# Batched matmul on one core: loads and stores moved from SyncE's DMA queue to GpSimd's, one packet per DMA engine

## The chip, the core and the metric

The kernel runs on one core of one Trainium2 chip. The metric is the device time of one execution in microseconds (us); the median of several runs is given. A profile of one execution comes with it.

## What is computed

For each of 32 batches the result is the matrix product of a 256 x 512 matrix and a 512 x 384 matrix, all in float32:

```python
batch, dim_i, dim_j, dim_k = 32, 256, 512, 384
x: (batch, dim_i, dim_j) float32
y: (batch, dim_j, dim_k) float32
return np.einsum('bij,bjk->bik', x, y).astype(np.float32)
```

In and out together, 54.5 MB pass between the chip's main memory (HBM) and the on-chip buffer (SBUF): 512 KB of x, 768 KB of y and 384 KB of results per batch.

## The kernel before

One batch is one step of the loop. `load(b)` brings x[b] and y[b] into SBUF with two DMAs: each of the 128 partitions gets two rows of x (4 KB, contiguous in HBM) and four rows of y (6 KB). `compute(b)` then does the following. ScalarE (ACT) and VectorE (DVE) cast the four row groups of y to float16, two each (`y_r`, L61 and L63). TensorE (PE) transposes x in eight 128 x 128 blocks by a multiplication with an identity matrix (L69), and DVE and ACT copy these from PSUM to SBUF as float16 (`xt_sb`, L71 and L73). Eight matmuls of 128 x 128 by 128 x 384 follow (L82), which add up four steps of j for each half of the rows, and ACT and DVE copy the two halves to `o_sb` (L91, L93). `store(b, o_sb)` writes 3 KB per partition back with one DMA (L97).

Loads run six batches ahead of the compute (`AHEAD`); x and y have nine buffers each, `o_sb` has eight. Before the loop the kernel issues the loads of batches 0 to 5; GpSimd (POOL) builds the identity matrix meanwhile. In the loop the load of batch b+6 is issued first, then the store of batch b. All 96 DMAs are issued by SyncE (SP), whose queue works in order: x(0), y(0), ..., x(6), y(6), store(0), x(7), y(7), store(1) and so on, with the stores of batches 25 to 31 at the end. A DMA is spread over the 16 DMA engines, eight partitions to each. The framework gives the DMAs eight completion semaphores in turn, so that from the ninth on each issue waits until the DMA eight places earlier has landed; a store waits for its `o_sb` as well, and a load for its buffer.

POOL does nothing after the identity matrix is built.

Of the kernel before, what the change touches and what calls it, by code (L numbers as in the profile page):

```python
# [1 line left out]

# [5 lines left out]


MM_DT = mybir.dt.float16  # L10
F32 = mybir.dt.float32
P = 128
AHEAD = 6


@with_exitstack
def kernel(
    ctx: ExitStack,
    tc: tile.TileContext,
    x: bass.AP,  # L20
    y: bass.AP,
    out: bass.AP,
):
    nc = tc.nc

    B, I, J = x.shape
    _, _, K = y.shape

    NI = I // P
    NJ = J // P  # L30

    const_pool = ctx.enter_context(tc.tile_pool(name="const", bufs=1))
    x_pool = ctx.enter_context(tc.tile_pool(name="x_pool", bufs=AHEAD + 3))
    y_pool = ctx.enter_context(tc.tile_pool(name="y_pool", bufs=AHEAD + 3))
    yr_pool = ctx.enter_context(tc.tile_pool(name="yr_pool", bufs=4))
    xt_pool = ctx.enter_context(tc.tile_pool(name="xt_pool", bufs=4))
    o_pool = ctx.enter_context(tc.tile_pool(name="o_pool", bufs=8))
    tpsum_pool = ctx.enter_context(tc.tile_pool(name="tpsum", bufs=4, space=bass.MemoryType.PSUM))
    opsum_pool = ctx.enter_context(tc.tile_pool(name="opsum", bufs=4, space=bass.MemoryType.PSUM))

    identity = const_pool.tile([P, P], F32)

    loaded = {}

    def load(b):


        x_sb = x_pool.tile([P, NI, J], F32, name="x_sb")
        y_sb = y_pool.tile([P, NJ, K], F32, name="y_sb")
        x_src = x[b].rearrange("(p r) j -> p r j", p=P)  # L50
        y_src = y[b].rearrange("(q t) k -> q t k", q=P)
        nc.sync.dma_start(out=x_sb, in_=x_src)  # L52
        nc.sync.dma_start(out=y_sb, in_=y_src)  # L53
        loaded[b] = x_sb, y_sb

    def compute(b):
        x_sb, y_sb = loaded.pop(b)
        y_r = yr_pool.tile([P, NJ, K], MM_DT, name="y_r")
        for t in range(NJ):
            if t % 2 == 0:  # L60
                nc.scalar.copy(y_r[:, t], y_sb[:, t])  # L61
            else:
                nc.vector.tensor_copy(y_r[:, t], y_sb[:, t])  # L63

        xt_sb = xt_pool.tile([P, NJ, NI, P], MM_DT, name="xt_sb")
        for t in range(NJ):
            t_ps = tpsum_pool.tile([P, NI, P], F32, name="t_ps")
            for r in range(NI):
                nc.tensor.transpose(t_ps[:, r], x_sb[:, r, t::NJ], identity)  # L69
            if t % 2 == 0:  # L70
                nc.vector.tensor_copy(xt_sb[:, t], t_ps)  # L71
            else:
                nc.scalar.copy(xt_sb[:, t], t_ps)  # L73

        o_sb = o_pool.tile([P, NI, K], F32, name="o_sb")
        o_ps = [
            opsum_pool.tile([P, K], F32, name=f"o_ps_{r}", tag="o_ps")
            for r in range(NI)
        ]
        for t in range(NJ):  # L80
            for r in range(NI):
                nc.tensor.matmul(  # L82
                    o_ps[r],
                    xt_sb[:, t, r],
                    y_r[:, t],
                    start=(t == 0),
                    stop=(t == NJ - 1),
                )
        for r in range(NI):
            if r % 2 == 0:  # L90
                nc.scalar.copy(o_sb[:, r, :], o_ps[r])  # L91
            else:
                nc.vector.tensor_copy(o_sb[:, r, :], o_ps[r])  # L93
        return o_sb

    def store(b, o_sb):
        nc.sync.dma_start(  # L97
            out=out[b].rearrange("(p r) k -> p r k", p=P), in_=o_sb
        )

    HEAD = 2
    load(0)
    load(1)
    make_identity(nc, identity)
    for b in range(HEAD, AHEAD):
        load(b)
    for b in range(B):
        if b + AHEAD < B:
            load(b + AHEAD)
        store(b, compute(b))  # L110


# [1 line left out]
_INS = ['x', 'y']  # L114
_OUTS = [((32, 256, 384), 'float32')]


# [23 lines left out]
```

## Time and profile before

| | |
|---|---|
| three runs | 137.07, 137.32, 137.32 us (median 137.32) |
| the profiled execution | 137.07 us, of which the span of the trace is 135.3 us |
| granted TensorE clock, mean | 0.992 of full speed |
| busy: PE, DVE, ACT, POOL | 85.9, 63.3, 68.9, 0.7 us |
| DMA | 54.64 MB, mean 404 GB/s over the span |
| from issue to landing, median | x 10.2 us, y 11.2 us, store 10.9 us |
| one issue on SP's queue | 0.33 us in the steady part, 0.38 to 0.46 at the start |

The profile is one execution's record. Busy time is the time in which an engine worked; an engine that isn't the bottleneck may idle for free. The slices divide the span into 40 equal parts, and the DMA row gives the busy share of the 16 DMA engines in tenths. The chain goes back from the last instruction to what released each step. Matmuls are pipelined and the ends of their records are modelled.

### The profile page before, as it was taken

Reading aid. Unit: us, or ns where it says so; the run is one execution under the profiler, and the core shown is the slowest. Engines: PE = TensorE matmul, PEld = TensorE weight load, DVE = VectorE, ACT = ScalarE, POOL = GpSimd, SP = SyncE. Lnnn points to the kernel's source line nnn. Section 1 sums busy time; section 2 is a strip of 40 time slices with the busy share of each in tenths; the row PEclk is TensorE's granted clock in tenths of the full one; section 3 lists DMA queues with packets and bytes.
Section 4 is the critical chain, followed back from the end, with each engine's and each line's share of the span. In section 5 each row is a group of like instructions: output and inputs, shape, how many; then the busy total and the mean of one; then the engine's idle time right before and its main releaser. Section 6 shows DMA issues by size and latency. Waiting matters only on the chain.

```text
span 135.3 us, 1733 instructions
## 1 busy us (share of the span) xinstructions
PE 85.9 (63%) x512; PEld 59.4 (44%) x512; DVE 63.3 (47%) x160; ACT 68.9 (51%) x161; POOL 0.7 (1%) x6
## 2 busy tenths in 40 slices
PE   0599777777745676565676565677565677565640
PEld 0457455555424454344454344454344454344420
DVE  0237555554436544446544456544446544446520
ACT  3246666664446454646454646454546444546520
POOL 2000000000000000000000000000000000000000
PEclk9999999999999999999999999999999999999996
DMA  4999999999999999999999999999999999999993
GB/s 166 408 420 418 417 415 397 410 412 421 410 423 414 416 420 421 421 427 413 419 420 419 419 420 422 424 416 419 420 419 423 414 417 419 422 421 416 413 392 149
DMA packets 13833, 54.64 MB, mean 404 GB/s; under 512 B 1536, under 2 KB 1536, under 8 KB 13824
## 3 DMA queue, kind: packets, MB, share of 16 engines
q1 hardware_dynamic: 13824, 54.53, 98.8%
q8 instruction: 4, 0.07, 0.2%
q14 instruction: 5, 0.04, 0.1%
HBM read 41.94 MB, written 12.58 MB: 403 GB/s over the span
## 4 chain that ended last, share of the span: by engine, by line
DMA 73%; PE 12%; DVE 5%; ACT 4%; SPq 2%; issue 1%; ACTq 0%
DMA y_sb<-in_y_dram 40%; DMA out_dram<-o_sb 33%; PE o_ps L82 10%; DVE xt_sb L71 3%; ACT y_r L61 3%; DVE y_r L63 2%; PE t_ps L69 1%; ACT o_sb L91 1%; SPq L52 1%; DVE o_sb L93 1%; SPq L53 1%; ACT xt_sb L73 0%; ACTq L61 0%
## 5 line engine op out<-in xcount | busy, mean ns | idle before, releaser
L82 PE MATMUL o_ps<-y_r,xt_sb 128*128 128x384 f16 x256 | 48.2, 331 | 35.2 <-ACT y_r L61 30.6
L82 PEld LDWEIGHTS <-xt_sb 128*128 128x128 f16 x256 | 25.0, 98 | 51.9 <-issue 35.7
L69 PE MATMUL t_ps<-identity,x_sb 128*128 128x128 f32 x256 | 39.2, 297 | 8.9 <-DMA x_sb<-in_x_dram 8.8
L69 PEld LDWEIGHTS t_ps<-identity,x_sb 128*128 128x128 f32 x256 | 34.7, 210 | 18.3 <-PE o_ps L82 13.4
L93 DVE COPY o_sb<-o_ps 128x384 f32<-128x384 f32 x32 | 17.8, 558 | 42.7 <-PE o_ps L82 42.7
L61 ACT CAST y_r<-y_sb 128x384 f16<-128x384 f32 x64 | 29.7, 510 | 13.3 <-DMA y_sb<-in_y_dram 13.3
L73 ACT CAST xt_sb<-t_ps 128x256 f16<-128x256 f32 x64 | 23.6, 373 | 18.5 <-PE t_ps L69 16.4
L91 ACT COPY o_sb<-o_ps 128x384 f32<-128x384 f32 x32 | 15.3, 479 | 29.0 <-PE o_ps L82 29.0
L63 DVE CAST y_r<-y_sb 128x384 f16<-128x384 f32 x64 | 20.1, 356 | 20.0 <-DMA y_sb<-in_y_dram 20.0
L71 DVE CAST xt_sb<-t_ps 128x256 f16<-128x256 f32 x64 | 26.6, 423 | 4.6 <-PE t_ps L69 4.1
L61 ACT ACT_TABLE_LOAD x1 | 1.3, 1283 | 0.7 <-PEq L125 0.7
masks.py:199 POOL TENSOR_SCALAR_AFFINE_SELECT identity<-identity 128x128 f32<-128x128 f32 x1 | 0.3, 294 | 0.1
masks.py:197 POOL MEMSET identity<- 128x128 f32 x1 | 0.2, 205 | 0.3 <-POOLq L125 0.3
L125 POOL MEMSET const-bfloat16-1.0<- 128x1 bf16 x1 | 0.1, 102 | 0.0
L125 POOL MEMSET const-uint8-127<- 128x1 uint8 x1 | 0.1, 102 | 0.0
L125 POOL MEMSET const-float32-0.0<- 128x1 f32 x1 | 0.1, 99 | 0.2 <-issue 0.2
L125 POOL MEMSET const-float32-1.0<- 128x1 f32 x1 | 0.1, 99 | 0.0
## 6 DMA issues: line engine op xcount, KB each, us to landing
y_sb<-in_y_dram SPq DMA_DIRECT2D x32, 768.0 KB, 11.2
x_sb<-in_x_dram SPq DMA_DIRECT2D x32, 512.0 KB, 10.2
out_dram<-o_sb SPq DMA_DIRECT2D x32, 384.0 KB, 10.9
```

The costliest lines, as they stand in the source:

```text
L52: nc.sync.dma_start(out=x_sb, in_=x_src)
L53: nc.sync.dma_start(out=y_sb, in_=y_src)
L61: nc.scalar.copy(y_r[:, t], y_sb[:, t])
L63: nc.vector.tensor_copy(y_r[:, t], y_sb[:, t])
L69: nc.tensor.transpose(t_ps[:, r], x_sb[:, r, t::NJ], identity)
L71: nc.vector.tensor_copy(xt_sb[:, t], t_ps)
L73: nc.scalar.copy(xt_sb[:, t], t_ps)
L82: nc.tensor.matmul(o_ps[r], xt_sb[:, t, r], y_r[:, t], start=(t == 0), stop=(t == NJ - 1),)
L91: nc.scalar.copy(o_sb[:, r, :], o_ps[r])
L93: nc.vector.tensor_copy(o_sb[:, r, :], o_ps[r])
L125: nc = _bacc.Bacc("TRN2", target_bir_lowering=False, num_devices=1)
```

## The change

The loads of batches 0 and 1 stay on SP's queue. All later loads and all stores are issued by POOL, in the same order as before, and with `single_packet=True`: the pieces that a DMA gives to one DMA engine (eight, one per partition) form one packet. The bytes, the tiles, the buffers and the compute stay as they were. The semaphores come in two groups now: SP's four DMAs use the first four of one group, and POOL's 92 DMAs go round eight of their own, so that POOL's first eight (loads 2 to 5) wait for no earlier DMA. POOL's issues stand behind the building of the identity matrix. The lines after the edit move by four: the casts are L65 and L67, the store L101.

```diff
-        nc.sync.dma_start(out=x_sb, in_=x_src)
-        nc.sync.dma_start(out=y_sb, in_=y_src)
+        if b < HEAD:
+            nc.sync.dma_start(out=x_sb, in_=x_src)
+            nc.sync.dma_start(out=y_sb, in_=y_src)
+        else:
+            nc.gpsimd.dma_start(out=x_sb, in_=x_src, single_packet=True)
+            nc.gpsimd.dma_start(out=y_sb, in_=y_src, single_packet=True)
         loaded[b] = x_sb, y_sb
...
     def store(b, o_sb):
-        nc.sync.dma_start(
-            out=out[b].rearrange("(p r) k -> p r k", p=P), in_=o_sb
+        nc.gpsimd.dma_start(
+            out=out[b].rearrange("(p r) k -> p r k", p=P), in_=o_sb, single_packet=True
         )
 
     HEAD = 2
```

## The prediction

> **What bounds the kernel now.** I read the page first (slices, queues, chain), then the DMA queue's issues in order of time, then short windows at both ends. The page says that the DMA engines are the bound:
>
> ```profile
> DMA  4999999999999999999999999999999999999993
> GB/s 166 408 420 418 417 415 397 410 412 421 410 423 414 416 420 421 421 427 413 419 420 419 419 420 422 424 416 419 420 419 423 414 417 419 422 421 416 413 392 149
> DMA packets 13833, 54.64 MB, mean 404 GB/s; under 512 B 1536, under 2 KB 1536, under 8 KB 13824
> ...
> q1 hardware_dynamic: 13824, 54.53, 98.8%
> ...
> DMA 73%; PE 12%; DVE 5%; ACT 4%; SPq 2%; issue 1%; ACTq 0%
> ```
>
> The engines are full in every slice but the first and the last, at about 419 GB/s, and 98.8% of their time is one queue. Of its 13,824 packets 1,536 are tiny (16 engines x 96 DMAs: the completions); the other 12,288 are one per partition and DMA. So each engine handles 24 data packets a batch (8 of 4 KB for x, 8 of 6 KB for y, 8 of 3 KB for a store) and 3 completions.
>
> The issue order, in the queue of SyncE (start, length, line):
>
> ```profile
> 95.57 0.33 SPq L52 DMA_DIRECT2D x_sb<-in_x_dram  x1
> 96.48 0.33 SPq L53 DMA_DIRECT2D y_sb<-in_y_dram  x1
> 97.75 0.34 SPq L97 DMA_DIRECT2D out_dram<-o_sb  x1
> 99.60 0.33 SPq L52 DMA_DIRECT2D x_sb<-in_x_dram  x1
> ```
>
> One batch takes 99.60 - 95.57 = 4.03 us, 4.05 over longer stretches (83.40 to 99.60 is four batches), with only 1.0 us of issuing. An issue waits for the DMA eight earlier, since there are eight completion semaphores. So seven DMAs are always queued behind the one that lands, some 7 x 1.35 = 9.5 us of work. Compute isn't the bound: when PE, DVE and ACT still lag (17.1 to 30 us of the chain) they do a batch in 3.28 us. A store is late only by order: that of batch 24 is issued at 114.02, while batch 31's results are ready at 130.67, so batch 24's, seven periods earlier, at about 102.3.
>
> Both ends (columns: window, its length, busy us of PE, PEld, DVE, ACT, POOL; then clock, DMA share, GB/s):
>
> ```profile
> 2.00:3.00 1.00, 0.00 (x0) 0.00 (x0) 0.00 (x0) 0.02 (x1) 0.00 (x0) 1.00 0.80 307
> 3.00:4.00 1.00, 0.00 (x0) 0.00 (x0) 0.00 (x0) 0.00 (x0) 0.00 (x0) 1.00 1.08 428
> ...
> 131.00:132.00 1.00, 0.00 (x0) 0.00 (x0) 0.00 (x0) 0.00 (x0) 0.00 (x0) 1.00 0.86 341
> 132.00:133.00 1.00, 0.00 (x0) 0.00 (x0) 0.00 (x0) 0.00 (x0) 0.00 (x0) 1.00 0.78 310
> 133.00:134.00 1.00, 0.00 (x0) 0.00 (x0) 0.00 (x0) 0.00 (x0) 0.00 (x0) 0.61 0.37 147
> ```
>
> The engines are full from about 2.5 us and run out one by one after 131. The sum below is against the profiled execution's own 137.07 us: span 135.30 and 1.77 around it. The three runs' median is 137.32.
>
> **Part 1, the packets.** 92 DMAs (30 x, 30 y, 32 stores, about 31 batches' worth) go from one packet per partition to one per engine, eight pieces in it. Bytes and their order stay. What a packet costs beside its bytes can be read from the trace's packet records: 3, 4 and 6 KB take 121, 159 and 234 ns. The line through them is 37.7 ns per KB; 8 ns don't scale. At that slope a batch's 104 KB per engine cost 3.92 us, and a batch takes 4.05, so 0.13 us is outside the bytes (27 packets at 5 ns, neighbours overlapping a little). If this goes with packets, 21 of 27 go, or 24 if a completion rides in its packet: 0.10 or 0.12 us a batch, over 31 batches 3.2 or 3.7 us. If it goes with the pieces, not the packets, 0. The fastest of the 40 slices (427 against 419) would make 2.4 us. A loss isn't excluded, since no row shows what POOL's queue costs the engines; I allow 1 us. I take -3.2, since the constant in the records is the nearest row.
>
> The Trainium skill ("DMA: Bandwidth & Descriptors", "Why small descriptors are slow (HBM only)") puts a fixed cost of about 3 cycles on each packet and says that joining them pays only at 256 B or below. With its 850 MHz that would be an estimate of 24 x 3.5 ns x 31 = 2.6 us; its second sentence speaks against the change, but at a queue this full even 2% shows.
>
> **Part 2, issuing from GpSimd.** 92 issues leave SP (0.33 us each) for POOL, otherwise empty after 1.30 us (0.7 us busy in all). The trace has no DMA issued by POOL. Below: SP's 0.33. Above: POOL's smallest instruction is 0.10 us, and one such step per DMA engine gives 1.6 us. I take 1.0, the middle. Three a batch are 3.0 us of 4.05. Each issue again waits for the DMA eight earlier; behind it stand the next loads and stores. The cover is the seven queued DMAs, 9.5 us against 1 us more of issue: cost nothing. It ceases at 1.35 us an issue, a third of a batch's 4.05, where the engines run dry (rival B).
>
> DVE's two y_r casts a batch (356 ns each) may meet these issues; neither 0.7 us more on POOL (3.7 of 4.05) nor a cast late by 1 us is on the path while compute has 0.77 us a batch to spare.
>
> The Trainium skill ("SBUF — State Buffer", "Who interferes with whom") says that a DVE copy or cast in a two-port mode locks GpSimd out, so descriptors wait. The 128x384 cast at 356 ns is shorter than the 128x256 one from PSUM at 423, which fits a faster mode; by the page part of these 0.7 us would be added to POOL's 3.0, still under 4.05.
>
> **Part 3, the start.** Loads 0 and 1 stay on SP; SP then has nothing to wait for. Loads 2 to 5 are eight DMAs free of waits on POOL, and x and y of load 6 follow as x(2), y(2) land. Then POOL stands at the store of batch 0, and loads 7 onward stand behind it. Now two queues feed the same engines at once, which this trace never shows. Before, x(0) landed at 4.16 and y(0) at 5.98. First bytes of POOL's x(2): 1.30 + 1.0 + 0.9 (SP's own lag, 0.74 to about 1.6) = 3.2 us.
>
> Bound one: the queues share bytes evenly. y(0) lands near 8.5, batch 0's store can issue near 13, and the 9.2 MB of loads 0 to 6 keep the engines busy to 1.8 + 9.2/0.418 = 23.8. Cost 0. Bound two: they alternate packet by packet, when each 6 KB packet of y(0) waits for a whole POOL packet of 32 or 48 KB (1.2 or 1.8 us). Eight of these and its own time are some 14 us; with one packet for the rest of x(0) and 1 us to land, y(0) is there near 20. Batch 0 took 10.66 - 5.98 = 4.7 us from there to its o_sb, so its store issues near 24.6 and moves 1.9 us later, near 26.5, while the engines ran dry at 23.8: cost 2.7 us, once, because compute at 3.28 us then gains on DMA at 3.95. I take the middle, +1.3, since no row decides it.
>
> The Trainium skill ("DMA: Bandwidth & Descriptors", "Queues, rings and completion order") has the second: engines go round their queues by whole packets. By it the sum below would be 1.4 us higher.
>
> **Part 4, the end.** The last store can issue only after batch 31's o_sb (130.67 now), and it landed 3.7 us later, behind stores 25 to 30. With POOL's longer issue 0 to 0.7 us shows; I take +0.3.
>
> **The sum.** 137.07 - 3.2 + 0 + 1.3 + 0.3 = 135.5 us, 1.1% less. Own range of this case: 133.4 (3.7 off, nothing given back) to 136.8 (3.2 off, 2.7 and 0.3 back: 136.9).
>
> **Rivals.**
> A, slower by little: the constant belongs to the pieces, not the packets, and the two queues at the start alternate. For it: the number of pieces per engine stays eight. Against: the constant is the same 8 ns for all three sizes, as a boundary would be. 137.07 + 2.7 + 0.3 = 140.1 with the whole start cost, 137.6 with a fifth of it at the start and no packet gain; 1 us more if the queue itself costs. Chance 0.23.
> B, slower by much: POOL becomes the bound. Place: the in-order queue of POOL from the first wait on. Price: 31 batches x 3 x (issue - 1.35). At 1.45 us 9.3 us more (146.4); at 1.6 it would be 23 us (160). It decides from 1.35. Against: the estimate of 1.0 and 25% room. Chance 0.15.
> C, no change that can be told: packet gain (2.4 by the slices, 3.2 by the records) and whole start cost (2.7) cancel, 136.8 to 137.3. Chance 0.09.
> D, the flag does nothing on these sizes, and POOL's queue delivers as SP's did: 137.1 to 137.5. Chance 0.03, mostly in "slower".
>
> **How the numbers follow.** The forecast has 0.50, with 133.4 to 136.8 as its own range. 0.2% (0.27 us) is about what a measurement of this kernel can tell from no change. Faster: 0.50, and 0.02 from C's edge: 0.52. Same: 0.08. Slower: A, B, the rest: 0.40. For 8 in 10 the range runs from 133.2 to 142.0: it takes in the forecast, A, C, D and B's beginning (1.40 us an issue), and leaves out the rest of B and a gain over 3.7.
>
> **What would show it.** In the profile after: data packets of the software queue at 3 per engine and batch, middle slices near 429 GB/s (1.704 MB in 3.95 us) if part 1 holds, 419 if not. POOL issues at 0.7 to 1.3 us with gaps between; solid POOL issues and DMA slices below 9 mean B. In the start, y(0) landing near 8.5 or near 20, and whether a DMA slice about 24 us has a hole. Wrong from the ground up would be middle slices under 415 with POOL idle: then the engines themselves go slower on this queue.

## The result and the profile after

The changed kernel took 141.86 us (median of four runs) against 137.22 us before on the same chip: a ratio of 1.036, with an interval of 1.029 to 1.043. It is slower by 4.6 us; the forecast was 135.5. The profiled execution took 141.8 us, of which the span is 140.0, so 1.8 us lie around the span, as before. All of the difference is inside the span.

First the page of the changed kernel, the same parts as were shown of before: slices, packets, queues, and the chain that ended last.

```profile
DMA  4999999999999999999999999999999999999800
GB/s 160 407 421 422 418 414 393 425 417 418 405 421 419 426 422 424 412 422 420 421 426 425 420 425 418 422 421 415 426 425 414 421 422 421 421 423 419 328 28 0
DMA packets 11785, 54.64 MB, mean 390 GB/s; under 512 B 1536, under 2 KB 1536, under 8 KB 11776
...
q0 software_dynamic: 11200, 51.91, 90.1%
q1 hardware_dynamic: 576, 2.62, 4.8%
...
DMA 77%; issue 8%; POOL 4%; PE 3%; DVE 1%; POOLq 1%
```

The middle slices are what they were: 393 to 426 GB/s (397 to 427 before), nines throughout. What is new is the end: the DMA row closes with 8, 0, 0 and the GB/s row with 328, 28, 0, where before it ran at 392 and 149 up to the last slice. A slice is 3.5 us here, so the engines that bound the kernel do nothing in its last two slices. The mean fell from 404 to 390 GB/s only because the span is longer. A share over the whole span only falls a little; the slices show at once where the time went.

The packets answer the first question of the prediction: 11,776 records below 8 KB and not 1,536 + 1,536. They are the pieces of before, with one exception: a store now has 64 records of 6 KB instead of 128 of 3 KB. So the flag did not make one packet of the eight pieces that go to a DMA engine.

The issues on POOL over one batch (start, length, engine and line, in brackets the idle time ahead and what ended it):

```profile
96.17 0.53 POOL L56 DMA_DIRECT2D x_sb<-in_x_dram  x1 [1.27 <-DMA y_sb<-in_y_dram]
96.88 0.53 POOL L57 DMA_DIRECT2D y_sb<-in_y_dram  x1 [0.18 <-issue]
98.38 0.55 POOL L101 DMA_DIRECT2D out_dram<-o_sb  x1 [0.98 <-DVE o_sb L97]
100.21 0.53 POOL L56 DMA_DIRECT2D x_sb<-in_x_dram  x1 [1.27 <-DMA y_sb<-in_y_dram]
```

One batch takes 100.21 - 96.17 = 4.04 us, and 4.04 over the four batches from 84.05 to 100.21, against 4.05 before. An issue costs 0.53 to 0.55 us, 1.6 us of the 4.04, with idle time between.

Both ends in short windows (window, its length, busy us of PE, PEld, DVE, ACT, POOL; clock, DMA share, GB/s):

```profile
2.00:3.00 1.00, 0.00 (x0) 0.00 (x0) 0.00 (x0) 0.02 (x1) 1.00 (x3) 1.00 0.84 324
3.00:4.00 1.00, 0.00 (x0) 0.00 (x0) 0.00 (x0) 0.00 (x0) 1.00 (x3) 1.00 1.00 399
...
132.00:133.00 1.00, 0.00 (x0) 0.00 (x0) 0.00 (x0) 0.00 (x0) 0.00 (x0) 1.00 0.80 326
133.00:134.00 1.00, 0.00 (x0) 0.00 (x0) 0.00 (x0) 0.00 (x0) 0.00 (x0) 1.00 0.35 141
134.00:135.00 1.00, 0.00 (x0) 0.00 (x0) 0.00 (x0) 0.00 (x0) 0.00 (x0) 0.55 0.00 0
...
139.00:140.00 1.00, 0.00 (x0) 0.00 (x0) 0.00 (x0) 0.00 (x0) 0.00 (x0) 0.50 0.00 0
```

The data end at 134 us in both kernels (in the packet records the last one ends at 133.97, before at 134.13). Before, the span was over at 135.3. Now six windows follow in which no engine and no DMA is busy. Who waits there is told by SP's waits; first before, then after (us in total, times, longest):

```profile
SPq L136 <- DMA out_dram<-o_sb: 3.2, 4, 0.9
...
SPq L136 <- PEq L136: 0.6, 2, 0.4
```

```profile
SPq L140 <- DMA out_dram<-o_sb: 131.8, 2, 126.3
SPq L140 <- PEq L140: 5.1, 2, 4.6
```

L136 and L140 are the same line, the one that leaves the program's context: there the engines meet at a final barrier. SP waits 4.6 us at it where it waited 0.4, and these 4.2 us are most of what was lost. The PE that is named is only the last one to give its sign; it waited itself. The chain of waits ends so (start, length, what):

```profile
127.66 3.47 issue
131.14 0.56 POOLq L140
```

After 131.70 the chain has nothing more to show, 8.3 us ahead of the end of the span. What stands there the view doesn't count as work. It is among the trace's own instruction records: GpSimd's DRAIN at L140, the instruction that closes its engine, begins at 131.14 and ends at 139.29. It takes 8.15 us. In the kernel before, where POOL has issued no DMA, the same record begins at 0.98 and ends at 1.37, as soon as the identity matrix is built; it takes 0.39 us and lies at the start of the kernel. SP saw the last store land at 134.47 (before 134.48), and from there 4.8 us pass until POOL is done with closing. From here on, *closing* stands for this record.

### The profile page after: what moved, and what is told of

Read it like the earlier page. It is cut to its first block, busy times and chain, and to the rows that moved or that the text cites. A ratio compares the mean times of both kernels' runs of the same rounds, so it can differ in the third digit from the quotient of the medians.

```text
span 140.0 us, 1737 instructions
## 1 busy us (share of the span) xinstructions
PE 86.8 (62%) x512; PEld 60.6 (43%) x512; DVE 62.3 (44%) x160; ACT 68.5 (49%) x161; POOL 50.2 (36%) x98
## 2 busy tenths in 40 slices
DMA packets 11785, 54.64 MB, mean 390 GB/s; under 512 B 1536, under 2 KB 1536, under 8 KB 11776
## 3 DMA queue, kind: packets, MB, share of 16 engines
q0 software_dynamic: 11200, 51.91, 90.1%
## 4 chain that ended last, share of the span: by engine, by line
DMA 77%; issue 8%; POOL 4%; PE 3%; DVE 1%; POOLq 1%
DMA y_sb<-in_y_dram 77%; POOL x_sb L56 3%; PE o_ps L86 2%; PE t_ps L73 1%; DVE y_r L67 1%; POOLq L140 0%; DVE xt_sb L75 0%; POOL identity masks.py:199 0%; POOL identity masks.py:197 0%; POOLq L56 0%; POOLq masks.py:199 0%; POOLq L57 0%; POOLq L129 0%
## 5 line engine op out<-in xcount | busy, mean ns | idle before, releaser
L86 PE MATMUL o_ps<-y_r,xt_sb 128*128 128x384 f16 x256 | 49.3, 337 | 32.6 <-ACT y_r L65 26.2
L73 PE MATMUL t_ps<-identity,x_sb 128*128 128x128 f32 x256 | 39.7, 300 | 10.6 <-DMA x_sb<-in_x_dram 7.8
L73 PEld LDWEIGHTS t_ps<-identity,x_sb 128*128 128x128 f32 x256 | 35.4, 210 | 19.3 <-PE o_ps L86 11.1
L65 ACT CAST y_r<-y_sb 128x384 f16<-128x384 f32 x64 | 29.6, 511 | 13.8 <-DMA y_sb<-in_y_dram 13.8
L101 POOL DMA_DIRECT2D out_dram<-o_sb x32 | 17.5, 548 | 36.1 <-DVE o_sb L97 20.5
L67 DVE CAST y_r<-y_sb 128x384 f16<-128x384 f32 x64 | 20.1, 356 | 20.3 <-DMA y_sb<-in_y_dram 20.3
L56 POOL DMA_DIRECT2D x_sb<-in_x_dram x30 | 16.1, 538 | 36.2 <-DMA y_sb<-in_y_dram 25.6
L75 DVE CAST xt_sb<-t_ps 128x256 f16<-128x256 f32 x64 | 26.1, 422 | 4.0 <-PE t_ps L73 3.6
L57 POOL DMA_DIRECT2D y_sb<-in_y_dram x30 | 15.9, 529 | 8.6 <-issue 4.0
```

What stands on the lines that cost most here:

```text
L56: nc.gpsimd.dma_start(out=x_sb, in_=x_src, single_packet=True)
L57: nc.gpsimd.dma_start(out=y_sb, in_=y_src, single_packet=True)
L86: nc.tensor.matmul(o_ps[r], xt_sb[:, t, r], y_r[:, t], start=(t == 0), stop=(t == NJ - 1),)
L101: nc.gpsimd.dma_start(out=out[b].rearrange("(p r) k -> p r k", p=P), in_=o_sb, single_packet=True)
```

## The experiments

The question is what GpSimd's closing does for 5 us after the last data, and which part of the change it hangs on. The expectations name three theories of it at first: T1, a fixed time from the last issue (7.6 us); T2, a fixed time after the last landing (4.8 us); T3, a time that grows with the number of DMAs that POOL has issued. Of each run the table below has the closing, read from the record of the DRAIN and from the completion records of POOL's queue. A completion is the 4-byte packet that each DMA engine sends behind its data.

### The flag alone

```diff
-            nc.gpsimd.dma_start(out=x_sb, in_=x_src, single_packet=True)
+            nc.gpsimd.dma_start(out=x_sb, in_=x_src)
...
```

(The same for y and for the store.)

> The changed kernel without single_packet. Three theories of the loss after the last transfer. T1: GpSimd's closing instruction (the DRAIN at the end, 8.15 us long in the changed kernel, 131.14 to 139.29) takes a fixed time from POOL's last issue. T2: it waits for POOL's last DMA to land (134.47) and then takes 4.8 us. T3: it takes some 0.09 us for each DMA that POOL issued (92). All three leave the loss where it is without the flag: about 141.9 us, with a DRAIN of about 8 us. The rival, that packets of eight pieces are handled worse by the DMA engines, expects less than 140. For the stores the changed kernel shows 64 packets of 6 KB where there were 128 of 3 KB; if the flag makes that, it goes back to 128 and the batch period from 4.03 to 4.05 us (0.6 us more in all); if the queue makes it, both stay.

It took 141.85 us, 1.032 of before (1.030 to 1.034), the time of the changed kernel. The page:

```profile
DMA packets 11785, 54.64 MB, mean 390 GB/s; under 512 B 1536, under 2 KB 1536, under 8 KB 11776
...
q0 software_dynamic: 11200, 51.91, 90.1%
```

These are the numbers of the changed kernel to the last packet; stores are joined to 6 KB here too, and the closing is 8.15 us again. So the flag leaves no trace in records or time, and joining a store's pieces is the doing of POOL's queue.

### One DMA on POOL, then two

```diff
-        nc.sync.dma_start(out=x_sb, in_=x_src)
+        (nc.gpsimd if b == HEAD else nc.sync).dma_start(out=x_sb, in_=x_src)
```

(against the kernel before; the second run also issues the store of the last batch from POOL)

> The kernel before with one change: x of batch 2 is loaded from POOL's queue, all else from SP's. T1, T2 and T3: the closing starts when POOL has nothing left, at about 2 us, and is over long before the end: 137.1 to 137.4. If any DMA on POOL's queue costs some 5 us once the kernel has ended (a step behind the last barrier): about 142.

> The kernel before with x of batch 2 and the store of batch 31 on POOL's queue, two DMAs in all. T1 (fixed from the last issue, 8.15 us from about 130.7): closing until about 138.9, some 141.3 us. T2 (4.8 us after the last landing at about 134.4): closing until about 139.2, some 141.7 us. T3 (0.09 us per DMA): two DMAs cost 0.2 us, some 137.5 us.

One early DMA: 137.38 us (ratio 0.9993 to 1.0029). The closing ran from 1.39 to 8.62 us, 0.43 us beyond that DMA's last completion, and lay beside the stream. With the last store there as well: 137.51 us (1.0002 to 1.0029); the closing ended at 134.95, 3.4 us after it began and 0.47 us after the last completion. T1 and T2 fall: both expected the loss back (141.3 and 141.7 us) as soon as POOL issued the last DMA. The closing waits for POOL's last completion, and what follows is short when there is little to close.

### The last store on SP

```diff
+        if b < B - 1:
+            nc.gpsimd.dma_start(out=dst, in_=o_sb, single_packet=True)
+        else:
+            nc.sync.dma_start(out=dst, in_=o_sb)
```

> The changed kernel with the store of batch 31 alone on SP's queue. POOL's last issue is then the store of batch 30, at about 127.1. T1 and T3 (8.15 us from there): DRAIN until about 135.3, span about 136, 137.8 us. T2 (that store lands at about 133.5, and 4.8 us follow): DRAIN until about 138.3, span about 139, 140.8 us.

139.64 us, 1.017 (1.015 to 1.019): 2.2 us better than the changed kernel, and neither of the two numbers expected. POOL's closing began at 126.98, its last completion came at 132.90, and it ended at 137.08, 4.2 us later. The closing ended 2.2 us earlier than in the changed kernel. Half of that (1.1 us) is POOL's last completion, which came earlier; the other half is the time behind it, 4.2 us against 5.3. SP's row names what is left at the barrier:

```profile
SPq L142 <- PEq L142: 3.3, 2, 2.9
```

### Fewer DMAs on POOL

```diff
-        if b < HEAD:
+        if b < ON_SP:
```

(ON_SP 17, then 25: the first 17 or 25 batches' loads come from SP, and POOL has 62 or 46 DMAs. The third run is the kernel before with only the stores of batches 0 to 20 issued by POOL. In a later run the bound is 4, and POOL has 88.)

> The changed kernel with the loads of batches 0 to 16 on SP's queue; POOL issues 62 DMAs (30 loads, 32 stores) in place of 92, the last one still the store of batch 31. Theory 'walk': the DRAIN goes through every DMA that POOL issued in the whole kernel, about 82 ns each (7.59 us from the last issue for 92). Then 62 x 0.082 = 5.1 us from the last issue at about 131.7: until 136.8, about 139.4 us. Rival 'fixed': a busy POOL queue costs 5.3 us after its last landing, however many DMAs it had: 141.9 us as with 92.

> The same with the loads of batches 0 to 24 on SP's queue; POOL issues 46 DMAs. 'Walk': 46 x 0.082 = 3.8 us from the last issue at about 131.7: until 135.5, about 138.1 us. 'Fixed': 141.9 us.

> The kernel before with the stores of batches 0 to 20 on POOL's queue, all loads and the stores of batches 21 to 31 on SP's. POOL has done its last DMA some 40 us before the end, so that its DRAIN is hidden under both theories. If POOL's queue joins a store's 128 pieces of 3 KB to 64 of 6 KB and each packet less saves 5 ns per engine, 21 stores save 21 x 4 x 5 ns = 0.4 us: 136.8 us against 137.25 before. If the joining saves nothing: 137.2.

62 DMAs: 140.16 us (1.017 to 1.024). 46: 139.43 us (1.012 to 1.019). 21 stores: 138.23 us (1.005 to 1.009). The theory of a fixed time, 141.9 us, is out, since both of the first two are well below. The closing after the last completion is 2.98, 2.34 and 1.36 us: with 0.43 and 0.47 for one and two DMAs that is a line, 0.43 + 0.041 for each further DMA (estimates 2.93, 2.28 and 1.25). T3 stands in this form.

The times are still 0.8 to 1.3 us above what was expected (139.4, 138.1 and 137.2). Some 0.5 to 0.6 of it is in the stream: the last store lands that much later than before. The page of the run with 21 stores:

```profile
GB/s 162 410 418 399 343 418 420 424 421 421 423 414 429 414 415 418 414 421 424 424 418 414 417 420 422 419 424 419 416 414 410 418 409 420 421 423 417 409 398 97
```

and, of the run with 62:

```profile
GB/s 185 414 413 363 367 410 429 420 427 411 425 419 419 422 415 423 414 426 417 418 416 412 415 420 420 423 421 424 417 418 422 425 419 416 424 416 423 417 208 0
```

POOL's first store is issued at 11.1 and 10.8 us beside a full queue of loads on SP, and the fourth and fifth slice fall to 343 to 399 GB/s; the last store is issued at 131.30, 131.80 and, with 46, 131.74 us, where before it was at 130.74. The run of 46 has the same dent (379 and 344). The dent is not the store's own traffic: by the packet records its first data move at 15.7 and 15.5 us, while the dent lies ahead of that (287 and 264 GB/s in the windows 13 to 15 us of the run with 21 stores, where before had 412 and 395), and it is SP's 6 KB pieces that are slow there, 369 ns on average from 13.5 to 14.5 us of the same run against 235. Why POOL's first store costs them that wasn't settled. In the run with 21 stores POOL's closing was over at 99.9 us, so nothing of its time is closing.

### Smaller pieces

```diff
-            nc.gpsimd.dma_start(out=y_sb, in_=y_src, single_packet=True)
+            nc.gpsimd.dma_start(out=y_sb, in_=y_src, single_packet=True, max_dma_last_dim=3072)
```

> The changed kernel with y's rows cut into pieces of 3 KB: still 92 DMAs on POOL's queue, but 30 of them with 16 pieces per DMA engine in place of 8 (976 pieces per engine in all against 736). 'Walk' over DMAs: the DRAIN ends 7.6 us after the last issue as before. A walk over pieces: 7.6 x 976 / 736 = 10.1 us. The stream is longer in both, by 30 x 8 packets x 5 ns = 1.2 us, so some 143.1 or 145.6 us; the length of the DRAIN after the last issue decides.

139.0 us (one run), and a surprise: with the same 92 DMAs, of which the 30 y loads are cut into twice the pieces, the closing shrank from 8.15 to 3.80 us, 0.96 of it after the last completion. (The packet records don't show the cut: there are 11,200 on POOL's queue as before, and y moves in 6 KB. It shows in y's issue, 0.71 us instead of 0.53.) SP's wait:

```profile
SPq L140 <- PEq L140: 0.8, 2, 0.5
```

Both expectations failed, 7.6 and 10.1 us from the last issue. (The stream itself was slower here, with the last store issued at 132.71 instead of 131.16.) So the number of DMAs alone doesn't set the closing. This gave the next theory, called "books" in the expectations: POOL keeps what it has issued in the buffer in which it writes its descriptors, until that is full and is used again; closing has to strike off what is left. On this theory the changed kernel's 92 DMAs fit into the buffer, and with the smaller pieces they don't quite. The rival, "walk": closing pays once for each DMA issued since the start, whatever the buffer.

### A smaller buffer

```diff
-    nc = _bacc.Bacc("TRN2", target_bir_lowering=False, num_devices=1)
+    nc = _bacc.Bacc("TRN2", target_bir_lowering=False, num_devices=1, dynamic_dma_scratch_size=2048)
```

(The changed kernel with its buffer at 2,048 bytes; then also with the last store on SP; then at 4,096 bytes. The fourth run has 88 DMAs and the buffer at full size.)

> The changed kernel with one number set at its launch: the buffer for POOL's descriptors is 2 KB per partition (some 127 descriptors per DMA engine, 14 DMAs of nine) in place of 16 KB (some 1,023; the 92 DMAs need 828, so that it never fills). Theory 'books': POOL keeps every DMA on its books until the buffer is full or the kernel closes, and the closing strikes them off at 41 ns each (0.43 us after the last landing with one DMA, 2.34 with 46, 2.98 with 62). Then at most 14 are left: 0.4 + 14 x 0.041 = 1.0 us after the last landing, in place of 5.3: about 137.6 us. Rival 'walk': the closing goes through all DMAs of the kernel, however large the buffer: 141.9 us. If the striking off in the middle of the kernel held POOL up, the batch period would be over 4.04 us.

> The same 2 KB buffer, and the store of batch 31 on SP's queue. 'Books': POOL's last DMA lands at about 133.3 and is closed by 134.3, when the store on SP lands too: 137.0 us, no slower than the kernel before (137.2). 'Walk': 139.6, as with the full buffer.

> The changed kernel with 4 KB per partition for the descriptors (some 255 per engine, 28 DMAs of nine). 'Books': at most 28 left at the end, 0.8 to 1.6 us after the last landing, depending on when the buffer was last cleared: 137.4 to 138.2 us. 'Walk': 141.9 us.

> The changed kernel with the loads of batches 0 to 3 on SP's queue: 88 DMAs on POOL's. The closing after the last landing lies on a line of 41 ns per DMA from 1 to 91 (0.43 to 4.17 us), but took 5.31 us with 92. On the line 88 give 4.0 us: 140.6 us. If the store of batch 31 as last DMA after so many adds a step of its own: 5.1 us, 141.7 us.

At 2,048 bytes the changed kernel takes 137.31 us, ratio 1.0007 (0.9995 to 1.0019) to before: the loss is gone. Its page and SP's waits (its profiled execution was the longest of its twelve, 138.14 us, with the last store issued 1.05 us later than in the changed kernel):

```profile
DMA  4999999999999999999999999999999999999963
...
q0 software_dynamic: 11200, 51.91, 92.6%
```

```profile
SPq L140 <- PEq L140: 0.6, 2, 0.5
```

The same 11,200 packets from the same queue, and SP's wait is down from 5.1 to 0.6 us. The closing ends 0.80 us after the last completion instead of 5.31. At 4,096 bytes the time is 137.14 us (one run) and the closing 0.77. "Walk" expected 141.9 in both and falls. With the last store on SP too it is 137.11 us, 1.0003 (0.9977 to 1.0029), the same as before within the interval. None of these beats the kernel before.

88 DMAs at full size took 141.39 us (1.028 to 1.031), nearer to 141.7 than to the line's 140.6. Together:

| kernel | DMAs on POOL | POOL's last completion | end of closing | after it, us | line, us |
|---|---|---|---|---|---|
| one early | 1 | 8.19 | 8.62 | 0.43 | 0.43 |
| early and last | 2 | 134.49 | 134.95 | 0.47 | 0.47 |
| 21 stores | 21 | 98.58 | 99.94 | 1.36 | 1.25 |
| loads from batch 25 on | 46 | 134.54 | 136.88 | 2.34 | 2.28 |
| loads from batch 17 on | 62 | 134.64 | 137.62 | 2.98 | 2.93 |
| loads from batch 4 on | 88 | 133.80 | 138.77 | 4.97 | 4.00 |
| last store on SP | 91 | 132.90 | 137.08 | 4.17 | 4.12 |
| changed kernel | 92 | 133.98 | 139.29 | 5.31 | 4.16 |
| smaller pieces | 92 | 135.53 | 136.49 | 0.96 | |
| buffer 4,096 bytes | 92 | 133.81 | 134.58 | 0.77 | |
| buffer 2,048 bytes | 92 | 134.69 | 135.49 | 0.80 | |
| the same, last store on SP | 91 | 132.90 | 133.94 | 1.04 | |

With the small buffer the traces show when POOL may be striking off. Two issues of y, one batch apart, at 2,048 bytes:

```profile
84.61 0.53 POOL L57 DMA_DIRECT2D y_sb<-in_y_dram  x1 [0.18 <-issue]
...
88.94 0.53 POOL L57 DMA_DIRECT2D y_sb<-in_y_dram  x1 [0.46 <-issue]
```

Counted from the last thing that an issue waits for (the issue before it, the landing of the DMA eight places earlier, a store's results), from the 22nd DMA on every seventh starts 0.22 to 0.30 us later than its like, and no other does; seven DMAs at 41 ns are 0.29. At 4,096 bytes it is the 29th (the buffer was expected to hold 28), 50th, 71st and 92nd, by 0.55 to 0.59 us. With the smaller pieces it is the 88th alone, by 1.8 us, and in the changed kernel and the run with 88 DMAs none from the 22nd on. That is what "books" asks for: in the runs with a short closing POOL has struck off DMAs before some of its issues, where the queued DMAs cover it. In both runs with 0.8 us the last such issue is the last store itself; with the last store on SP it comes six DMAs before POOL's last one, and the closing takes 1.04 us, 0.24 more, which is six times 41 ns. How many are struck off at a time these runs don't show.

Two rows, 88 and 92, lie 1.0 and 1.1 us above the line. A closing in two passes over the DMAs would fit them: a first pass of 0.2 us and 41 ns for each DMA from the start of the closing, which is free as long as POOL's last completion comes later, and the pass of the line behind both. In these rows the last completion comes 2.8 us after the start, and the first pass takes 4.0 and 3.8, 1.1 and 1.0 us more. With 62 DMAs it takes 2.7, and with the last store on SP the completion comes 5.9 us after the start; there it is hidden. This is an estimate fitted to the table; no run was made to test it. What the runs show is enough without it: the closing grows with the DMAs on POOL's queue while the buffer holds them all, and is short once the buffer is too small for them, with the stream unchanged.

## Why the prediction was wrong, step by step

**The step that failed: the base of the sum.** It took the 137.07 us of before as a base, and with it the 0.8 us between the last landing and the end of the span, as if the end of a program were the same whichever engine had issued its DMAs. Part 4 looked no further than the last landing, and sized only the issue of the last store. That part was as good as right: SP sees the last landing at 134.47 against 134.48, so +0.3 was 0. Behind it came 4.7 us (140.0 - 134.47 against 135.3 - 134.48) which no step and no rival named. They come from the closing of GpSimd, which ends 5.3 us after its last completion when 92 DMAs are in its buffer, and 0.8 us after it when the buffer is too small to hold them. "Wrong from the ground up" was put as middle slices under 415; they were at 420 on average (43 to 83 us), and the time was wrong all the same. By the terms as measured the sum is 137.07 - 0.2 (to the end of the data) + 0 + 0 + 4.9 (from there on, 140.0 - 133.97 against 135.3 - 134.13) = 141.8, as measured.

**Part 1, -3.2 us, was about -0.2.** It rested on 21 of 27 packets per engine and batch going. The loads kept their pieces and only stores were joined: 4 go, at the prediction's 5 ns each 0.02 us a batch and 0.6 over 31. The last batch's results were done at 130.61 us (130.67 before) and the last data ended 0.16 us earlier. The price of 5 ns isn't refuted, the count was wrong: that the flag would join anything was read off the diff, and the run without the flag shows that it joined nothing. Rival D had its first half right (the flag does nothing) at a chance of 0.03, and failed on its second. (The sign to look for was also miscounted: 1.704 MB in 3.95 us are 431 GB/s, not 429.)

**Part 2, cost 0, held, with a size off.** An issue was put at 1.0 us between 0.33 and 1.6 and is 0.53:

```profile
L101 POOL DMA_DIRECT2D out_dram<-o_sb x32 | 17.5, 548 | 36.1 <-DVE o_sb L97 20.5
...
L67 DVE CAST y_r<-y_sb 128x384 f16<-128x384 f32 x64 | 20.1, 356 | 20.3 <-DMA y_sb<-in_y_dram 20.3
L56 POOL DMA_DIRECT2D x_sb<-in_x_dram x30 | 16.1, 538 | 36.2 <-DMA y_sb<-in_y_dram 25.6
...
L57 POOL DMA_DIRECT2D y_sb<-in_y_dram x30 | 15.9, 529 | 8.6 <-issue 4.0
```

All three are far below rival B's 1.35 us, and the idle time of POOL ends on DMAs and results, so B is out. The cast that was to meet these issues is at 356 ns, as before. 32 of the 64 casts overlap an issue in time and take 354 ns on average, so no lock between the two shows.

**Part 3, +1.3 us, was 0.** The data of 3 to 43 us flow at 415 GB/s in both kernels, and no slice shows a hole. Bound one came nearer, for a reason that the prediction didn't have: POOL's first data moved only at 5.5 us, 3.4 us after the end of its first issue (1.47 to 2.15), when x(0) and most of y(0) were in. The estimate of 3.2 us for these first data was 2.3 us short. y(0)'s cast began at 6.14 us against 5.99. What shared the engines was y(1), which was cast from 12.69 instead of 9.36, with no harm, since the engines were full.

From 6 to 10 us, when both queues fed the engines, the packet records count 159 pieces of POOL's queue and 177 of SP's, about one to one. The Trainium skill ("DMA: Bandwidth & Descriptors", "Queues, rings and completion order") has an engine drain a whole packet of some 9 to 17 descriptors before it changes queues. As the prediction applied it, to POOL's side alone, it would have been one to eight; the records say about even shares, and don't show in what units.

The same page ("Latency and other measured facts") puts the first byte of a DMA from GpSimd at about 1 us. Here that fits the last store, whose first data move 1.2 us after its issue begins (0.6 after it ends), with the engines nearly free. It doesn't fit beside loads on SP's queue: POOL's first load takes 3.4 us from the end of its issue (3.1 in the run with one early DMA), and in the run with 21 stores, which had nothing else on POOL's queue, the first took 3.9 us and each of the 20 others 3.1 to 3.4.

**Rivals A and C.** A had the right sign, slower at 137.6 to 140.1 us, but from a start cost, and there was none: had the time fallen there, it would have been luck. C's two terms, the packet gain and the start cost, were both about nothing.

## What to carry to other kernels

A sum that is made against a base ends where the program ends, not where the data end: when DMAs move to another engine, ask what that engine does when it closes, and read the slices and the barrier's waits behind the last landing. With up to 62 DMAs on GpSimd's queue the closing cost here 0.4 us and 41 ns for each further one after its last completion, and 5.3 us with 92; a smaller buffer takes nearly all of that away (141.86 to 137.31 us), and the last DMA on another queue a part of it (139.64). And a flag's effect on packets is counted in one look at the records, before anything is built on it.

## What was not expected of the hardware

- GpSimd's closing: 8.15 us with 92 DMAs in the buffer, of which 5.3 after the last completion; 0.39 us, at the start of the kernel, when it issues none. More pieces, or a smaller buffer, make it shorter.
- With the buffer at 2,048 bytes every seventh issue of POOL starts 0.22 to 0.30 us later, and at 4,096 bytes every 21st 0.55 to 0.59 us; the kernel's time is that of before in both.
- A store from POOL's queue moves in 64 pieces of 6 KB where SP's queue has 128 of 3 KB, with the flag and without it. Loads keep one piece per partition.
- A DMA of POOL with nothing ahead of it on POOL's queue delivers its first data 3.1 to 4.0 us after the end of its issue when SP's loads are running, and the last store, with the engines nearly free, after 0.6 us.
- When POOL issued its first store at 11 us beside a full queue of loads on SP, DMA fell to some 340 to 400 GB/s for two slices (6.8 us), ahead of that store's first data; POOL's first load at the very start did not do that.
